# Moving 224 stores of computed results from SyncE's queue to GpSimd's

## The chip, the cores and the metric

The kernel runs on one core of a Trainium2 chip. The metric is the device time of one execution in microseconds; the kernel before takes 2093.06 us, the median of three runs (2092.97 to 2096.44). The engines are TensorE (PE: matmuls; PEld is its weight load, which overlaps), VectorE (DVE), ScalarE (ACT), GpSimd (POOL) and SyncE (SP). DMA transfers are issued from the queue of an engine; this kernel issues from SP and, for some stores, from ACT. SP computes nothing: its queue holds only DMA issues, which it takes in order, each waiting for what it needs.

## The reference

A sequence of 2048 rows of 1024 (plus 16 meta rows in front) goes through one layer of a hybrid decoder in float32:

```python
s = layer_norm(concat(meta, x))                       # 2064 x 1024
u = s @ w_in                                          # conv value, conv gate, q, k, v, r, gate-down
conv_out = silu(layer_norm(causal_conv31(a * sigmoid(gate)) + conv_b))
gla_out  = rms_norm(gla_chunked(q, k, v, log_g)) * silu(r)
s = layer_norm(alpha * s + concat(conv_out, gla_out) @ w_out)
f = square(relu(s @ w_ff1)) @ w_ff2                   # 1024 -> 4096 -> 1024
s = layer_norm(alpha * s + f)                         # output: the 2048 rows after the meta rows
```

## The kernel before, in words

The 2048 rows are four blocks of 512. A float32 product is made of three matmuls: `split` (L189 to L191) copies the high part of an operand on ACT and subtracts it on DVE, which gives a high and a low tile. The kernel is a program of *units* (one product or a few, on PE), each with *loads* (a weight's DMA and its split) that are emitted as many units ahead as there are free slots in a ring of ten weight slots (`wp`), and of *sides* (input normalization, conv, attention, tails), generators that are stepped between units in proportion to the units' costs. A scheduler then gives every engine's instructions their final order and sets the semaphores; each engine works through its own list in order. A tile that is reused waits for the readers and the stores of its last use.

The stages in order of time, from the trace: input normalization, w_in products, gate, conv (on DVE, L723) and attention (0 to 625 us); w_out of blocks 0 and 1 (627 to 705); FF1 of half 0, that is of blocks 0 and 1 (705 to 1035); FF2 of half 0 (1035 to 1345); w_out of blocks 2 and 3 (1376 to 1452); FF1 of half 1 (1452 to 1771); FF2 of half 1 (1771 to 2082), last normalization and the output's stores.

FF1 is done with seven products for eight (a scheme after Strassen). The weight's columns make 16 groups. For groups 0 to 9 two of the seven products are made in advance (the *front*), and their results wait in DRAM (`a1d` and `hor`); in the main part such a group has five products, 6, 5, 7, 3, 4, and `reload` (its DMAs are L1020 and L1022) brings the two results back as `a` and `h`. Groups 10 to 15 have seven products. For each group two pieces of the weight, `w1r` number 0 and 1 (512 KB each, L964), take slots of the ring; DVE combines them in place and splits them (L971, then L191, giving `wop`), and `s`, a third combination, takes a small tile. `wop` of product 4, the last, reads piece 1. After the products DVE (L1034) makes combinations `p`, `u`, `h`, `s` for FF2, and `put` (L1004) stores each into `hor`; FF2 loads them as `lr` (L1125).

What leaves the core's memory in between: `s0d` (normalized input, L304), `hd` (gated conv input, L602, its halo L606, the meta rows L620), `mixd` (attention result `go`, L704, and conv result `cy`, L753), `s1d` (normalized residual, L842, L887) and `hor`. All of these are read back later, by SP loads: `xin` and `wacc` (L833), `hin` (L717), `mraw` (L825), `lr`. Their stores are issued on SP, in the order in which the scheduler puts them; those of `put` that are marked `late` are emitted one unit later than their result by `prog.defer`.

POOL fills constants at the start and makes the power step (x^-0.5, L215 and L243) of every normalization: DVE gives the variance, POOL the power, DVE and ACT apply it, and in the conv normalization PE then transposes (L744) what ACT made (`cn`, L741).

Of the kernel before, what the change touches and what calls it, by code (L numbers as in the profile page):

```python
# [17 lines left out]
P = 128  # L18
# [3 lines left out]
SUB = 512  # L22
# [4 lines left out]
CT = DCONV // P  # L27
# [118 lines left out]
def hymba_kernel(ctx: ExitStack, tc: tile.TileContext, x, meta, ln_in_g, ln_in_b, w_in, small, gate_up,  # L146
# [143 lines left out]
    def prep_tile(s, tt):  # L290
        if s or tt == 0:
            load_x(s, tt)
        t = xin[s, tt]
        if s == 0 and tt == 0:
            nc.sync.dma_start(out=A.g, in_=ln_in_g.partition_broadcast(P))
            nc.sync.dma_start(out=A.b, in_=ln_in_b.partition_broadcast(P))
        yield
        st = stats_bn(t) if s == 0 and tt < NBN else stats_act(t, None, pa, "sg")
        if s == 0 and tt == 0:
            prog.pre(4)  # L300
            load_x(0, 1)
        yield
        yield from ln_apply(t, st, A.g, A.b)
        nc.sync.dma_start(out=s0d[s][tt], in_=t)  # L304
        yield from transpose_split(t, xt[s], tt)
        if s == 0 and tt == 0:
            prog.pre(RING - 4)
            consts()
# [131 lines left out]
    def win_units(s):  # L440
# [157 lines left out]
        def val_evac(i, m, ps):  # L598
            ct = i * 2 + m
            h = pa.tile([P, SUB], F32, tag="h", name="h", bufs=2)  # L600
            nc.vector.tensor_tensor(out=h, in0=ps, in1=sig[ct], op=ALU.mult)
            nc.sync.dma_start(out=hd[s][ct][:, HALO:], in_=h)  # L602
            if s:
                hdone.add((s, ct))
            if s + 1 < NSUB:
                nc.sync.dma_start(out=hd[s + 1][ct][:, :HALO], in_=h[:, SUB - HALO:])  # L606

        sigm = {}

# [5 lines left out]
        def valm_evac(i, m, ps):  # L615
            ct = i * 2 + m
            h = pa.tile([P, HALO], F32, tag="hm", name="hm", bufs=2)
            nc.vector.memset(h[:, :HALO - NMETA], 0.0)
            nc.vector.tensor_tensor(out=h[:, HALO - NMETA:], in0=ps[:, :NMETA], in1=sigm[ct], op=ALU.mult)
            nc.sync.dma_start(out=hd[0][ct][:, :HALO], in_=h)  # L620
            hdone.add((0, ct))

        def gate_val():
# [25 lines left out]
    def gla(s):  # L649
        w = W[s]  # L650
        for c in range(TT):
# [49 lines left out]
                nc.tensor.transpose(tp[:, h * P:(h + 1) * P], og[:, h * P:(h + 1) * P], ident)  # L701
            go = pa.tile([P, 512], F32, tag="go", name="go", bufs=1)
            nc.scalar.activation(go, tp, AF.Identity, scale=sm[:, SM_GG:SM_GG + 1])
            nc.sync.dma_start(out=mixd[s][1][:, :, lo:lo + P], in_=go.rearrange("p (h t) -> p h t", h=NH))  # L704
            yield

    GLA_N = TT * 7
# [3 lines left out]
    def conv(s):  # L711
# [15 lines left out]
        for tt in range(TT):  # L727
            tp = tp_tile()
            for ct in range(CT):
                nc.tensor.transpose(tp[:, ct * P:(ct + 1) * P], accs[ct][:, tt * P:(tt + 1) * P], ident)  # L730
            st = stp.tile([P, 1, 6], F32, tag="cbn", name="cbn")
            nc.vector.bn_stats(st[:, 0], tp)
            mv = stp.tile([P, 2], F32, tag="mv", name="mv")
            nc.vector.bn_aggr(mv, st)
            rs = stp.tile([P, 1], F32, tag="rs", name="rs")
            rstd_of(rs, mv[:, 1:2], 1)
            nm = stp.tile([P, 1], F32, tag="nm", name="nm")
            nc.vector.scalar_tensor_tensor(out=nm, in0=mv[:, 0:1], scalar=-1.0, in1=rs, op0=ALU.mult, op1=ALU.mult)
            yield
            n = cv.tile([P, 512], F32, tag="cn", name="cn", bufs=2)  # L740
            nc.scalar.activation(n, tp, AF.Identity, bias=nm[:, 0:1], scale=rs[:, 0:1])  # L741
            tb = tp_tile()
            for ct in range(CT):
                nc.tensor.transpose(tb[:, ct * P:(ct + 1) * P], n[:, ct * P:(ct + 1) * P], ident)  # L744
            yield
            y = cv.tile([P, 512], F32, tag="cy", name="cy", bufs=1)
            for ct in range(CT):
                nc.scalar.activation(y[:, ct * P:(ct + 1) * P], tb[:, ct * P:(ct + 1) * P], AF.Identity,
                                     bias=sm[:, SM_CLB + ct:SM_CLB + ct + 1], scale=sm[:, SM_CG + ct:SM_CG + ct + 1])
            sg = cv.tile([P, 512], F32, tag="cn", name="csg", bufs=2)  # L750
            nc.scalar.activation(sg, y, AF.Sigmoid)
            nc.vector.tensor_tensor(out=y, in0=y, in1=sg, op=ALU.mult)
            nc.sync.dma_start(out=mixd[s][0][:, :, tt * P:(tt + 1) * P], in_=y.rearrange("p (c t) -> p c t", c=CT))  # L753
            yield

    CONV_N = CT * CW + TT * 3
# [78 lines left out]
    def wout_units(s, late=None):  # L835
        sums = {}

        def post(tt):
            a = wacc[s, tt]
            for _ in ln_apply(a, stats_act(a, sums[tt], rawp, "raw"), B.g1, B.b1):  # L840
                pass
            nc.sync.dma_start(out=s1d[s][tt], in_=a)  # L842
            if tt == 0:
                st1[s] = xt_pair()
            for _ in transpose_split(a, st1[s], tt):
                pass
# [33 lines left out]
    def back_units(half, stats, X):  # L880
# [3 lines left out]
        def norm(tt):  # L884
            t = wacc[b, tt]
            yield from ln_apply(t, stats[tt], B.g1, B.b1)
            nc.sync.dma_start(out=s1d[b][tt], in_=t)  # L887

        def turn(tt):
            t = wacc[b, tt]  # L890
# [51 lines left out]
    def ff1s_units(half, stats, f2):  # L942
# [61 lines left out]
        def put(g, i, t, late=False):  # L1004
            o = hor[half][g // GP][i - 1][:, g % GP, :]
            if late:
                prog.defer(1, lambda: nc.sync.dma_start(out=o, in_=t))
            else:
                nc.scalar.dma_start(out=o, in_=t)

# [361 lines left out]
```

## Time and profile before

| | |
|---|---|
| median of three runs | 2093.06 us |
| the profiled execution | 2097.01 us, span 2095.3 us |
| busy share: PE, PEld, DVE, ACT, POOL | 96%, 79%, 79%, 48%, 4% |
| DMA | 409.39 MB, 195 GB/s over the span |
| weight loads of PE in FF1, half 0 (705 to 1035 us) | 256.74 us of 330 |
| in FF1, half 1 (1452 to 1771 us) | 249.65 us of 319 |
| in FF2, half 0 (1035 to 1345 us) | 251.09 us of 310 |

A busy share is an average over stages with different limits, and PE's matmuls are pipelined, so its 96% still contains short losses; the busy time or the count of its weight loads in a window shows them better. What SP waits for is a wait of a queue: it costs only where something that it issues afterwards comes too late for an engine that then makes PE late. SP, ACT and POOL each take their DMA issues in order.

### The profile page before, as it was taken

To read this page: it belongs to the slowest core of one execution; us is meant where nothing else is said; L and a number is where in the kernel's file an instruction comes from. 1 tells how busy PE (TensorE), PEld (TensorE's weight loads), DVE (VectorE), ACT (ScalarE), POOL (GpSimd) and SP (SyncE) were. 2 spreads that over 40 slices of the span, in tenths; PEclk is the share of its full clock that TensorE was granted. 3 is DMA by queue.
4 is the path that set the end of the run, shared out by engine and by line. 5 is a ranking of instruction groups with operands and counts; after the bars stand their busy time and mean duration, and the time that the engine had idled before them with its cause. 6 is when DMAs were issued, how large, how long until landed. Compare 5 with 4: busy or idle time off the path is not lost. (4 is left out here: it accounts for less than half of the span.)

```text
span 2095.3 us, 26293 instructions
## 1 busy us (share of the span) xinstructions
PE 2021.2 (96%) x9144; PEld 1645.3 (79%) x9144; DVE 1650.6 (79%) x2662; ACT 1002.6 (48%) x1717; POOL 82.1 (4%) x97
## 2 busy tenths in 40 slices
PE   7999999999999999999999999999999999899997
PEld 5878878878777877778788788777777788788886
DVE  6699979989998777776699999579878766544776
ACT  4563474554543554455653434455644554444332
POOL 1000100100000000000000000011000000000001
PEclk9999999999999999999999999999999999999999
DMA  6533534534346656554899877277666548865772
GB/s 204 177 105 93 158 106 122 161 86 134 106 138 209 194 171 217 195 181 161 284 330 389 308 252 269 72 245 251 193 204 204 183 147 283 311 213 188 250 243 79
DMA packets 245285, 409.39 MB, mean 195 GB/s; under 512 B 21424, under 2 KB 115856, under 8 KB 245152
## 3 DMA queue, kind: packets, MB, share of 16 engines
q1 hardware_dynamic: 226144, 368.91, 53.8%
q10 hardware_dynamic: 19008, 38.81, 4.9%
q8 instruction: 72, 1.18, 0.2%
q14 instruction: 61, 0.50, 0.1%
HBM read 297.29 MB, written 110.35 MB: 195 GB/s over the span
## 5 line engine op out<-in xcount | busy, mean ns | idle before, releaser
L723 DVE SCALAR_TENSOR_TENSOR cacc<-hin,sm,cacc 128x512 f32<-128x512 f32 x480 | 344.9, 747 | 2.0
L1211 PE MATMUL mm<-op 128*128 128x512 f32 x544 | 213.6, 393 | 7.5 <-ACT op L190 7.5
L190 ACT CAST wsl<-raw 128x512 fp32r<-128x512 f32 x224 | 136.6, 620 | 164.0 <-PE mm L389 36.5
L1212 PE MATMUL mm<-op 128*128 128x512 f32 x544 | 212.9, 391 | 0.0
L1213 PE MATMUL mm<-op 128*128 128x512 f32 x544 | 211.7, 391 | 0.0
L190 ACT CAST op<-wr 128x1024 fp32r<-128x1024 f32 x92 | 92.4, 1050 | 221.9 <-PE mm L1213 161.4
L191 DVE TENSOR_TENSOR op<-wr,op 128x1024 fp32r<-128x1024 f32 x92 | 109.0, 1221 | 79.4 <-ACT op L190 79.4
L191 DVE TENSOR_TENSOR wsl<-raw,wsl 128x512 fp32r<-128x512 f32 x224 | 150.9, 686 | 21.8 <-ACT wsl L190 21.4
L1000 PE MATMUL gl<-x,wop 128*128 128x512 f32 x384 | 152.2, 398 | 8.0 <-DVE a L1034 2.9
L387 PE MATMUL mm<-xt,wsl 128*128 128x512 f32 x384 | 152.7, 398 | 0.0
L388 PE MATMUL mm<-xt,wsl 128*128 128x512 f32 x384 | 151.3, 394 | 0.0
L389 PE MATMUL mm<-xt,wsl 128*128 128x512 f32 x384 | 151.1, 394 | 0.0
L1001 PE MATMUL gl<-x,wop 128*128 128x512 f32 x384 | 150.6, 392 | 0.0
L1002 PE MATMUL gl<-x,wop 128*128 128x512 f32 x384 | 150.2, 392 | 0.0
L1211 PEld LDWEIGHTS mm<-op 128*128 128x128 f32 x544 | 102.8, 189 | 30.1 <-ACT op L190 8.3
L190 ACT CAST wop<-w1r 128x512 fp32r<-128x512 f32 x152 | 91.1, 616 | 68.5 <-DVE w1r L971 39.8
L1212 PEld LDWEIGHTS mm<-op 128*128 128x128 f32 x544 | 102.8, 189 | 21.3
L1213 PEld LDWEIGHTS mm<-op 128*128 128x128 f32 x544 | 102.4, 188 | 21.7 <-DVE op L191 0.2
L191 DVE TENSOR_TENSOR op<-lr,op 128x1024 fp32r<-128x1024 f32 (+1 forms) x92 | 105.0, 1175 | 16.6 <-ACT op L190 16.5
L191 DVE TENSOR_TENSOR wop<-w1r,wop 128x512 fp32r<-128x512 f32 x152 | 103.8, 687 | 16.3 <-ACT wop L190 15.7
L1000 PE MATMUL mm<-xt,wop 128*128 128x512 f32 x256 | 100.7, 396 | 5.7 <-ACT a L1040 5.7
L1001 PE MATMUL mm<-x,wop 128*128 128x512 f32 x256 | 101.2, 395 | 0.9 <-DVE x L191 0.9
(277 smaller groups left out, 4795.1 us busy)
## 6 DMA issues: line engine op xcount, KB each, us to landing
wr<-in_w_dram SPq DMA_DIRECT2D x120, 512.0 KB, 6.1
lr<-hor SPq DMA_DIRECT2D x108, 512.0 KB, 6.0
raw<-in_w_in_dram SPq DMA_DIRECT2D x160, 256.0 KB, 2.9
w1r<-in_w_dram SPq DMA_DIRECT2D x64, 512.0 KB, 5.2
wr<-td SPq DMA_DIRECT2D x40, 512.0 KB, 5.2
raw<-in_w_out_dram SPq DMA_DIRECT2D x64, 256.0 KB, 3.8
hor<-s SPq DMA_DIRECT2D x64, 256.0 KB, 3.0
raw<-in_w_dram SPq DMA_DIRECT2D x40, 256.0 KB, 3.9
```

Source lines behind the costliest of these rows:

```text
L190: nc.scalar.copy(hi, src)
L191: (eng or nc.vector).tensor_tensor(out=lo, in0=src, in1=hi.bitcast(F32), op=ALU.subtract)
L387: nc.tensor.matmul(ps, wh, mov(k, 0), start=(k == 0), stop=False)
L388: nc.tensor.matmul(ps, wh, mov(k, 1), start=False, stop=False)
L389: nc.tensor.matmul(ps, wl, mov(k, 0), start=False, stop=(k == KD - 1))
L723: nc.vector.scalar_tensor_tensor(out=acc, in0=h[:, j:j + SUB], scalar=wc(j), in1=acc, op0=ALU.mult, op1=ALU.add)
L1000: nc.tensor.matmul(ps, wh, X[i][:, k, 0, :], start=start and k == 0, stop=False, skip_group_check=not start)
L1001: nc.tensor.matmul(ps, wh, X[i][:, k, 1, :], start=False, stop=False, skip_group_check=not start)
L1002: nc.tensor.matmul(ps, wl, X[i][:, k, 0, :], start=False, stop=(k == 3), skip_group_check=not start)
L1211: nc.tensor.matmul(ps, lh, rt[n][:, p, 0, :], start=(q == 0 and p == 0), stop=False)
L1212: nc.tensor.matmul(ps, lh, rt[n][:, p, 1, :], start=False, stop=False)
L1213: nc.tensor.matmul(ps, ll, rt[n][:, p, 0, :], start=False, **ends)
```

## The change

Nine lines that issued a store on SP issue it on POOL: 16 stores `s0d` (512 KB each), 16 `hd` (256 KB), 12 halos, 4 of the meta rows, 16 `go` and 16 `cy` (256 KB), 16 `s1d` (512 KB), and 128 `hor` (256 KB: 64 from `s`, 32 from `u`, 32 from `h`). The last ones are no longer deferred. The stores of the output (L1290, L1292) and the loads stay on SP, and ACT's stores stay on ACT.

```diff
--- before.py
+++ after.py
@@ -301,7 +301,7 @@
             load_x(0, 1)
         yield
         yield from ln_apply(t, st, A.g, A.b)
-        nc.sync.dma_start(out=s0d[s][tt], in_=t)
+        nc.gpsimd.dma_start(out=s0d[s][tt], in_=t)
         yield from transpose_split(t, xt[s], tt)
         if s == 0 and tt == 0:
             prog.pre(RING - 4)
@@ -599,11 +599,11 @@
             ct = i * 2 + m
             h = pa.tile([P, SUB], F32, tag="h", name="h", bufs=2)
             nc.vector.tensor_tensor(out=h, in0=ps, in1=sig[ct], op=ALU.mult)
-            nc.sync.dma_start(out=hd[s][ct][:, HALO:], in_=h)
+            nc.gpsimd.dma_start(out=hd[s][ct][:, HALO:], in_=h)
             if s:
                 hdone.add((s, ct))
             if s + 1 < NSUB:
-                nc.sync.dma_start(out=hd[s + 1][ct][:, :HALO], in_=h[:, SUB - HALO:])
+                nc.gpsimd.dma_start(out=hd[s + 1][ct][:, :HALO], in_=h[:, SUB - HALO:])
 
         sigm = {}
 
@@ -617,7 +617,7 @@
             h = pa.tile([P, HALO], F32, tag="hm", name="hm", bufs=2)
             nc.vector.memset(h[:, :HALO - NMETA], 0.0)
             nc.vector.tensor_tensor(out=h[:, HALO - NMETA:], in0=ps[:, :NMETA], in1=sigm[ct], op=ALU.mult)
-            nc.sync.dma_start(out=hd[0][ct][:, :HALO], in_=h)
+            nc.gpsimd.dma_start(out=hd[0][ct][:, :HALO], in_=h)
             hdone.add((0, ct))
 
         def gate_val():
@@ -701,7 +701,7 @@
                 nc.tensor.transpose(tp[:, h * P:(h + 1) * P], og[:, h * P:(h + 1) * P], ident)
             go = pa.tile([P, 512], F32, tag="go", name="go", bufs=1)
             nc.scalar.activation(go, tp, AF.Identity, scale=sm[:, SM_GG:SM_GG + 1])
-            nc.sync.dma_start(out=mixd[s][1][:, :, lo:lo + P], in_=go.rearrange("p (h t) -> p h t", h=NH))
+            nc.gpsimd.dma_start(out=mixd[s][1][:, :, lo:lo + P], in_=go.rearrange("p (h t) -> p h t", h=NH))
             yield
 
     GLA_N = TT * 7
@@ -750,7 +750,7 @@
             sg = cv.tile([P, 512], F32, tag="cn", name="csg", bufs=2)
             nc.scalar.activation(sg, y, AF.Sigmoid)
             nc.vector.tensor_tensor(out=y, in0=y, in1=sg, op=ALU.mult)
-            nc.sync.dma_start(out=mixd[s][0][:, :, tt * P:(tt + 1) * P], in_=y.rearrange("p (c t) -> p c t", c=CT))
+            nc.gpsimd.dma_start(out=mixd[s][0][:, :, tt * P:(tt + 1) * P], in_=y.rearrange("p (c t) -> p c t", c=CT))
             yield
 
     CONV_N = CT * CW + TT * 3
@@ -839,7 +839,7 @@
             a = wacc[s, tt]
             for _ in ln_apply(a, stats_act(a, sums[tt], rawp, "raw"), B.g1, B.b1):
                 pass
-            nc.sync.dma_start(out=s1d[s][tt], in_=a)
+            nc.gpsimd.dma_start(out=s1d[s][tt], in_=a)
             if tt == 0:
                 st1[s] = xt_pair()
             for _ in transpose_split(a, st1[s], tt):
@@ -884,7 +884,7 @@
         def norm(tt):
             t = wacc[b, tt]
             yield from ln_apply(t, stats[tt], B.g1, B.b1)
-            nc.sync.dma_start(out=s1d[b][tt], in_=t)
+            nc.gpsimd.dma_start(out=s1d[b][tt], in_=t)
 
         def turn(tt):
             t = wacc[b, tt]
@@ -1004,7 +1004,7 @@
         def put(g, i, t, late=False):
             o = hor[half][g // GP][i - 1][:, g % GP, :]
             if late:
-                prog.defer(1, lambda: nc.sync.dma_start(out=o, in_=t))
+                nc.gpsimd.dma_start(out=o, in_=t)
             else:
                 nc.scalar.dma_start(out=o, in_=t)
```

Three places show how the instructions move. First SP's list in the main part of FF1, half 0, in two periods of groups with five products. In the names `hor_0_6_146` is a DRAM tile, `w1r` the weight pieces, `a` and `h` the reloads; in brackets are the semaphores an instruction waits for (DMAHW: an earlier DMA of SP or ACT; DMASW: one of POOL; Activation is ACT). Before:

```order
L1007 DMA hor_0_6_146<-s_7408 128x512 [waits DVE_49]
L1007 DMA hor_0_4_144<-u_7338 128x512 [waits DMAHW7_49,DVE_49]
L964 DMA w1r<-in_w_dram 128x4x256 [waits DMAHW1_49,PE_49]
L1007 DMA hor_0_5_145<-h_7216 128x512 [waits DMAHW2_49,DVE_49]
L1007 DMA hor_0_2_142<-s_7432 128x512 [waits DMAHW3_49,DVE_49]
L964 DMA w1r<-in_w_dram 128x4x256 [waits DMAHW4_49,PE_49,Activation_49]
L1022 DMA h_7576<-hor_1_0_147 128x512 [waits DMAHW5_49,DMAHW2_49]
L1020 DMA a_7814<-a1d_7_219 128x512 [waits DMAHW6_49,DMAHW0_49,Activation_49]
L1007 DMA hor_0_6_146<-s_7528 128x512 [waits DVE_49]
L964 DMA w1r<-in_w_dram 128x4x256 [waits DMAHW1_49,PE_49]
L1007 DMA hor_0_4_144<-u_7458 128x512 [waits DMAHW3_49,DVE_49]
L1007 DMA hor_0_5_145<-h_7336 128x512 [waits DMAHW4_49,DVE_49]
```


After, at the same groups:

```order
L964 DMA w1r<-in_w_dram 128x4x256 [waits DMAHW4_49,PE_49]
L964 DMA w1r<-in_w_dram 128x4x256 [waits DMAHW6_49,DMAHW0_49,DVE_49]
L1020 DMA a_7935<-a1d_8_220 128x512 [waits DMAHW5_49,DVE_49]
L1022 DMA h_7697<-hor_1_0_147 128x512 [waits DMASW6_49]
L964 DMA w1r<-in_w_dram 128x4x256 [waits DMAHW2_49,PE_49]
L964 DMA w1r<-in_w_dram 128x4x256 [waits DMAHW6_49,DMAHW4_49,DVE_49]
L1020 DMA a_8055<-a1d_9_221 128x512 [waits DMAHW3_49,DVE_49]
L1022 DMA h_7817<-hor_1_0_147 128x512 [waits DMASW2_49]
L964 DMA w1r<-in_w_dram 128x4x256 [waits DMAHW0_49,PE_49]
L964 DMA w1r<-in_w_dram 128x4x256 [waits DMAHW4_49,DMAHW2_49,DVE_49]
```


The stores are gone, and of the two `w1r` loads of a group the first waits for PE alone, the second for DVE: for the `wop` of product 4 of the group before, the last reader of the slot that it takes.

Second, DVE's list around the change from one group to the next in the same part. `wop<-w1r,wop` is the low half of a split; the last of them ahead of `s_7746<-w1r` is that of product 4. Before:

```order
L191 TENSOR_TENSOR wop<-s_7626,wop 128x4x128 [waits Activation_49]
L1034 TENSOR_TENSOR h_7456<-u_7578,h_7456 128x512 [waits DMAHW0_49,DVE_49]
L191 TENSOR_TENSOR wop<-w1r,wop 128x4x128 [waits Activation_49]
L1034 TENSOR_TENSOR s_7672<-a_7454,h_7456 128x512 [waits DMAHW3_49,DVE_49,Activation_49]
L1034 TENSOR_TENSOR u_7698<-a_7574,gl 128x512 [waits DMAHW7_49]
L191 TENSOR_TENSOR wop<-w1r,wop 128x4x128
L971 TENSOR_TENSOR s_7746<-w1r 128x512 [waits DMAHW3_49]
L1034 TENSOR_TENSOR p_7719<-p_7719,gl 128x512 [waits DMAHW0_49,PE_49,Activation_49]
L1034 TENSOR_TENSOR p_7719<-p_7719,a_7574 128x512 [waits DVE_49]
L971 TENSOR_TENSOR w1r<-w1r 128x4x128 [waits DMAHW0_49]
```


After:

```order
L1034 TENSOR_TENSOR a_7455<-a_7455,gl 128x512 [waits DVE_49,PE_49]
L1034 TENSOR_TENSOR s_7649<-h_7457,u_7579 128x512 [waits DMASW1_49,Activation_49]
L1034 TENSOR_TENSOR u_7579<-u_7579,p_7599 128x512 [waits DVE_49]
L191 TENSOR_TENSOR wop<-w1r,wop 128x4x128 [waits Activation_49]
L1034 TENSOR_TENSOR h_7457<-u_7579,h_7457 128x512 [waits DMASW6_49,DVE_49]
L191 TENSOR_TENSOR wop<-w1r,wop 128x4x128 [waits Activation_49]
L1034 TENSOR_TENSOR s_7675<-a_7455,h_7457 128x512 [waits DMASW3_49,DVE_49]
L1034 TENSOR_TENSOR u_7699<-a_7575,gl 128x512 [waits DMAHW3_49]
L971 TENSOR_TENSOR s_7746<-w1r 128x512 [waits DMAHW2_49]
L971 TENSOR_TENSOR w1r<-w1r 128x4x128 [waits DMAHW4_49,DVE_49,PE_49]
```


The `wop` of product 4 stood behind the last combination `s` and the next `u`; now it stands ahead of both. The first use of piece 1 (`w1r<-w1r`) stood behind two combinations `p`; now it follows the `s` from `w1r` at once. From one first use of piece 1 to the `wop` of product 4 there are fourteen instructions after the first. Instructions that write a stored tile now wait for a POOL store (DMASW) of an earlier group.

Third, POOL's list in the input stage, at the conv normalization of block 0. Before, power steps alone (`rs` and `rr` are the variances of the normalizations and of the attention):

```order
L215 TENSOR_TENSOR rr<-rr,nhalf 128x4 [waits DVE_49]
L215 TENSOR_TENSOR rs<-rs,nhalf 128x1 [waits DVE_49,Pool_49] x2
L243 TENSOR_TENSOR rs<-rs,nhalf 128x1 [waits DVE_49,Pool_49]
L215 TENSOR_TENSOR rs<-rs,nhalf 128x1 [waits DVE_49,Pool_49]
L215 TENSOR_TENSOR rs<-rs,nhalf 128x1 [waits DVE_49,Activation_49]
L215 TENSOR_TENSOR rr<-rr,nhalf 128x4 [waits DVE_49]
L243 TENSOR_TENSOR rs<-rs,nhalf 128x1 [waits DVE_49]
```


After:

```order
L215 TENSOR_TENSOR rs<-rs,nhalf 128x1 [waits DVE_49,Pool_49]
L753 DMA mixd_0_232<-cy 512x1x128 [waits DMASW2_49,DVE_49]
L215 TENSOR_TENSOR rs<-rs,nhalf 128x1 [waits DVE_49,Pool_49]
L243 TENSOR_TENSOR rs<-rs,nhalf 128x1 [waits DVE_49,Pool_49]
L304 DMA s0d_3_103<-xin 128x1024 [waits DMASW3_49,DVE_49]
L215 TENSOR_TENSOR rs<-rs,nhalf 128x1 [waits DVE_49,Pool_49]
L753 DMA mixd_0_232<-cy 512x1x128 [waits DMASW4_49,DVE_49]
L704 DMA mixd_1_233<-go 512x1x128 [waits DMASW5_49,Activation_49]
L215 TENSOR_TENSOR rs<-rs,nhalf 128x1 [waits DVE_49,Pool_49]
L753 DMA mixd_0_232<-cy 512x1x128 [waits DMASW6_49,DVE_49]
```


The same power steps now stand between stores, each of which waits for the tile that it stores and for the POOL store eight before it.

## Rows read from the trace of the kernel before

**Rows 1.** The page, busy time and share of the span by engine.

```profile
PE 2021.2 (96%) x9144; PEld 1645.3 (79%) x9144; DVE 1650.6 (79%) x2662; ACT 1002.6 (48%) x1717; POOL 82.1 (4%) x97
```

**Rows 2.** Windows: start:end, us; busy time (and count) by engine, clock, DMA share, GB/s.

```profile
850.00:925.00 75.00, 72.53 (x311) 57.72 (x310) 56.57 (x92) 35.91 (x64) 0.00 (x0) 1.00 0.57 193
925.00:1025.00 100.00, 99.93 (x440) 81.13 (x438) 62.13 (x100) 52.62 (x90) 0.55 (x1) 1.00 0.55 186
```

**Rows 3.** Waits of PE: line, releaser: total us, times, longest.

```profile
PE tp L744 <- ACT cn L741: 7.5, 10, 1.4
PE mm L1211 <- ACT op L190: 7.5, 2, 6.1
```

**Rows 4.** Waits of DVE.

```profile
DVE s L971 <- DMA w1r<-in_w_dram: 47.3, 27, 4.1
```

**Rows 5.** Waits of SP's queue.

```profile
SPq L1007 <- DVE s L1034: 188.0, 56, 12.5
...
SPq L964 <- DVE wop L191: 74.1, 11, 10.4
...
SPq L1022 <- DMA hor<-h: 53.3, 17, 4.5
```

**Rows 6.** Timeline of SP in FF1: start, duration, line, operation.

```profile
860.13 0.38 SPq L964 DMA_DIRECT2D w1r<-in_w_dram  x1
...
864.65 0.38 SPq L1007 DMA_DIRECT2D hor<-s  x1
865.13 0.45 SPq L964 DMA_DIRECT2D w1r<-in_w_dram  x1
```

**Rows 7.** Timeline of DVE in the same period; idle time before, with releaser, in brackets.

```profile
866.61 0.69 DVE L971 TENSOR_TENSOR s<-w1r 128x512 f32<-128x512 f32 x1 [2.68 <-DMA w1r<-in_w_dram]
...
870.58 0.69 DVE L971 TENSOR_TENSOR w1r<-w1r 128x512 f32<-128x512 f32 x1 [2.68 <-DMA w1r<-in_w_dram]
...
879.70 0.68 DVE L191 TENSOR_TENSOR wop<-w1r,wop 128x512 fp32r<-128x512 f32 x1
```

**Rows 8.** Timeline of DVE: group 3 and group 10 of half 0.

```profile
792.80 0.69 DVE L971 TENSOR_TENSOR s<-w1r 128x512 f32<-128x512 f32 x1 [2.50 <-DMA w1r<-in_w_dram]
...
895.16 0.69 DVE L971 TENSOR_TENSOR s<-w1r 128x512 f32<-128x512 f32 x1 [0.20 <-DMA w1r<-in_w_dram]
```

**Rows 9.** The line of the `w1r` loads: time from issue to landing.

```profile
DMA to landing us min/median/max: 3.5/5.2/7.4
```

**Rows 10.** Timeline of SP, from FF1 to FF2 in half 1.

```profile
1780.21 0.32 SPq L1007 DMA_DIRECT2D hor<-s  x1
...
1781.11 8.72 SPq L1125 DMA_DIRECT2D lr<-hor  x5
```

**Rows 11.** Timeline of DVE at the same place.

```profile
1785.25 1.23 DVE L1161 TENSOR_TENSOR wr<-wr 128x1024 f32<-128x1024 f32 x1 [5.07 <-DMA wr<-in_w_dram]
```

**Rows 12.** Timeline of ACT, then PE, at w_out of blocks 2 and 3.

```profile
1367.14 2.64 ACT L190 CAST xt<-mraw 128x512 fp32r<-128x512 f32 x4 [8.31 <-DMA mraw<-mixd]
...
1381.38 0.73 PE L860 MATMUL gl<-wsl,xt 128*128 128x512 f32 x2 [1.43 <-ACT wsl L190]
```

**Rows 13.** Timelines of POOL (its longest step), then of one conv normalization.

```profile
186.57 2.05 POOL L215 TENSOR_TENSOR rr<-rr,nhalf 128x4 f32<-128x4 f32 x1 [81.37 <-DVE rr L214]
...
262.18 0.55 POOL L215 TENSOR_TENSOR rs<-rs,nhalf 128x1 f32<-128x1 f32 x1 [9.60 <-DVE rs L214]
...
262.76 0.16 DVE L738 SCALAR_TENSOR_TENSOR nm<-mv,rs 128x1 f32<-128x1 f32 x1 [0.72 <-POOL rs L215]
263.01 0.78 ACT L741 ACTIVATE cn<-tp,nm,rs 128x512 f32<-128x512 f32 x1 [0.78 <-DVE nm L738]
...
263.84 0.33 PE L744 MATMUL tp<-ident,cn 128*128 128x128 f32 x1 [0.75 <-ACT cn L741]
```

**Rows 14.** Timelines of DVE and POOL at the start.

```profile
10.04 1.61 DVE L348 CAST wgd<-qbd 128x96 fp32r<-128x96 f32 x1
...
9.67 0.99 POOL L345 MEMSET at<- 128x512 f32 x2
```


## Prediction

> **What bounds the kernel now.** I read the page first: TensorE (PE) is busy in 96% of the span, so what can be won at most is what PE loses, and a store matters only where its queue makes PE late or stops doing so [rows 1]. A table of windows shows where. In 925 to 1025 us, where every group of FF1 has seven products, PE starts 438 weight loads in 100 us, one per 0.228 us. In 850 to 925 us, mostly groups with five products, it starts 310 in 75 us, one per 0.242 us: 6% is lost there [rows 2]. PE's own waits are short everywhere, 7.5 us in the largest entries [rows 3], but VectorE (DVE) waits 47.3 us for the pieces `w1r` of the FF1 weight, the same stretch seen from the engine that makes PE's operands [rows 4].
>
> Then I read SyncE's queue (SP), which holds all the stores that the change moves. It stood 188.0 us behind stores of `s`, 74.1 us behind the slots of `w1r`, 53.3 us behind stores that had to land before a reload [rows 5]. These are waits of a queue, not of PE, so they are no gain as they stand. One period tells what they do: the load of the first `w1r` (I call it r0) is issued at 860.13 us, right behind a store of `s`, and the second (r1) at 865.13 us, right behind the next store of `s` [rows 6]. DVE uses them at 866.61 and 870.58 us, each after idling 2.68 us for it [rows 7]. So stores do hold loads up, in the groups with five products, and the steady ones start 14.62 us apart ((895.16 − 792.80)/7) [rows 8]. Sixty matmuls at 0.228 us are 13.7 us: 0.92 us per group is the most that PE can get back. There are seven such periods in each half.
>
> **The change, part by part.** 224 stores leave SP for POOL; nothing is added or removed in arithmetic, and the bytes stay.
>
> *FF1, 128 stores.* On SP each group keeps two loads and two reloads. r0 now waits only for PE's product 5 of two groups before, so it is no longer late. r1 is different: the order shows that it waits for the last `wop` of the group before, because it takes the slot of that group's own r1. That is a loop by itself: from DVE's first use of r1 to that `wop` are 14 instructions. DVE issues them 0.608 us apart when it doesn't wait (870.58 to 879.70 us is 15 steps), so 14 steps and one last instruction of 0.68 us are 9.2 us [rows 7]. Then comes the load itself. In the period shown r1 took 865.13 to 870.58, 5.45 us; the view of that line gives 3.5 at least, 5.2 in the median and 7.4 at most [rows 6, 7, 9]. With r0's load gone well ahead, r1 shares the DMA engines with stores and a reload only, so I take 5.05 us, a little under the median. The loop is then 14.25 us. Gain: 14 periods × (14.62 − 14.25) = **−5.2 us**. The bounds are PE's floor, 14 × 0.92 = −12.9 us, and a landing of 6.0 us, a loop of 15.2, +8 us. So the stall moves from r0 to r1, and most of what was lost stays lost.
>
> The first three groups of each half keep the same order on SP, and I cost them at nothing.
>
> *FF1 to FF2.* Ahead of the first loads of FF2, SP issues at 1780.21 us the last store, then a piece `wr`, and from 1781.11 the `lr` loads of `hor`; DVE gets `wr` 5.07 us late [rows 10, 11], and PE pays 6.1 us for it, the longest wait of the entry for line L1211 [rows 3]. The `lr` loads still wait for the last `s` by the reuse of a tile; only the store and `wr` in front go away, 1781.11 − 1780.21 = 0.9 us. Two halves: **−1.8 us** (bounds 0 and −6).
>
> *The last block's `mixd`.* The loads of `mraw` that open w_out of blocks 2 and 3 read what `cy` stored; ACT waits 8.31 us for them at 1367.14, and later PE 1.43 us behind the weights that were queued after them [rows 12]. A store that POOL issues is on a chain to PE here. SP's slot for a store is 0.38 us [rows 6]; POOL's price for issuing one is shown by nothing in this trace. I bound it by 0.38 from below and by the longest small instruction of POOL, 2.05 us, from above [rows 13], and take 1.0, a little under their middle. With a landing later by a few tenths: **+1.3 us** (0 to +3).
>
> *POOL in the input stage, 80 stores, and s1d, 16.* POOL was 4% busy [rows 1] with the small power step of each normalization. Now these steps stand in order behind stores, and a store waits for its tile and occupies POOL. In the conv normalization such a step stands between DVE, ACT and PE: POOL 262.18, DVE 262.76, ACT 263.01, PE 263.84, with PE idle 0.75 us [rows 13]. PE waited 7.5 us in ten of the places like it [rows 3], so there a delay is paid nearly in full. Of the 16 conv chains perhaps a quarter find a store of 1.0 us in the way, half done: 4 × 0.5 = 2.0, and half a microsecond for the other normalizations, which have PE work before them: **+2.5 us** (bounds 0, and 16 × 1.0 = +16 where every chain meets one).
>
> What takes cover: 64 stores per half in FF1 at 1.0 us each are 4 us of POOL per period of 14; nothing else runs on POOL there, and if that cover fails DVE waits for the `s` and `u` tiles that the stores free.
>
> The sum: −5.2 − 1.8 + 1.3 + 2.5 = −3.2 us. The profiled execution took 2097.0 us, 3.9 above the median 2093.06; it becomes 2093.8, and on the scale of the median **2089.9 us**. A difference under 0.2% (4.2 us) can't be told from none, so this lies just inside "no change".
>
> The trace shows two engines holding one another: DVE's small cast, 128×96, took 1.61 us at 10.04 while POOL's fills ran [rows 14], and POOL's power step takes from 0.55 to 2.05 us [rows 13]. The Trainium skill, page "SBUF — State Buffer", section "Who interferes with whom", has a rule that speaks against this change: POOL writes the descriptors of its DMAs, and is locked out while DVE runs an instruction in a two-port mode; it advises SP or ACT as issuer. The rows agree that the two engines meet; no row here shows a store on POOL, so the rule enters as the third rival.
>
> **The rivals.**
>
> *PE becomes the bound in FF1 (faster).* If r1 alone in the queue lands in 4.5 us or less, the loop is at most 13.7 us, PE's floor, and 14 × 0.92 = 12.9 us come back: −12.9 − 1.8 + 1.3 + 2.5 = −10.9, **2082 us**. For it: the shortest landings are 3.5 us [rows 9]. Against: the median is 5.2, and the four stores of a group now start as soon as their results are there, just while r1 is on its way.
>
> *POOL's order holds the normalizations (slower).* One mechanism: a power step stands behind a store whose tile is not ready, or whose issue is long. It decides from the point where the delay exceeds the slack of a chain, 0 for the ten conv places where PE waits already. With all 16 conv chains 0.8 us later (one store in the way) and 1.0 us for each of six others, that is 12.8 + 6 = 18.8 in place of 2.5; −5.2 − 1.8 + 1.3 + 18.8 = +13.1, **2106 us**. For it: POOL's rows after the change alternate steps and stores. Against: the order follows the times at which the work is due, and 80 stores in 600 us are one in 7.5 us.
>
> *Stores on POOL slow DVE or themselves (slower).* If each of the four stores of a group costs DVE what the cast at 10.04 lost, 1.61 − 0.68 (taking DVE's usual instruction, an upper price for so small a cast) = 0.9 us, and half of them fall into r1's loop, it grows by 1.8 us: 14 × 1.8 = +25 on the sum, **2115 us**. For it: rows 14. Against: a step of POOL that ran beside long DVE instructions was itself the one that grew.
>
> *The stores don't matter.* That the change does what it says is shown by the order; but if r1 lands as before in 5.4 us, the loop is 14.6 us and the sum is +2: 2095 us, inside the main case.
>
> **How the numbers follow.** The forecast with its own range 2085 to 2097: 0.48, of it 0.17 below 2088.9. PE the bound: 0.24. POOL's order: 0.20. POOL against DVE: 0.08. Faster by over 0.2%: 0.24 + 0.17 = 0.41; slower: 0.28 less 0.03 for weak forms of it, 0.25; the same 0.34. The range leaves a tenth on each side: from 2079 (PE bound with both changes of stage gaining in full, −1 us each more) to 2107.
>
> **What would show it.** Right: SP's waits behind `s` gone; DVE's wait before `s` from `w1r` near nothing, and its wait before the first `w1r` sum 2 us or more; periods of 14.0 to 14.5 us; the `tp` wait in L744 within 3 us of 7.5. Periods of 13.7 prove the first rival; L744 at 15 us or more, with POOL steps starting late behind stores, the second; DVE instructions longer than 0.69 us beside POOL's stores the third. The forecast is wrong as a whole if r1's load is not what DVE waits for.

## The result, and the profile after

The changed kernel is slower: 2160.28 us, median of four runs (2157.57 to 2164.77), beside 2094.75 us for the kernel before on the same chip; the ratio is 1.0298, with a 95% interval of 1.0279 to 1.0318. The forecast was 2089.9 us, with a range up to 2107.

The page's line of busy times answers to [rows 1]; under it is the queue that the change added:

```profile
PE 2041.2 (95%) x9144; PEld 1656.7 (77%) x9144; DVE 1649.6 (76%) x2662; ACT 1004.6 (47%) x1717; POOL 213.2 (10%) x321
...
q0 software_dynamic: 19200, 63.17, 8.2%
```

PE's busy time rose by 20 us, though its work is the same, and the span by 64.5. Four of the waits of PE follow; two of them answer to [rows 3] (line, releaser: total us, times, longest):

```profile
PE gl L1000 <- DVE p L1034: 38.5, 17, 3.6
PE tp L744 <- ACT cn L741: 12.1, 12, 3.2
...
PE mm L1211 <- ACT op L190: 8.6, 3, 7.7
...
PE gl L860 <- DVE wacc L867: 5.7, 5, 2.5
```

The first is new: 38.5 us in FF1, in line 1000, behind DVE's `p` (0.8 us before). The stages say the same. Each number is the distance between the first or last matmuls of lines 860, 1000 and 1211 in one trace, in us; two stages that no edit reached differ between traces by up to 2.6 us (w_out, 111.6 and 114.2 with the same order), so smaller differences in this table say nothing:

| kernel | input | w_out 0, 1 | FF1 half 0 | FF2 half 0, w_out 2, 3 | FF1 half 1 | rest |
|---|---|---|---|---|---|---|
| before | 593.5 | 111.6 | 328.9 | 412.1 | 324.3 | 324.9 |
| after | 597.3 | 113.7 | 353.3 | 420.1 | 348.3 | 327.1 |

FF1 lost 24.4 and 24.0 us of the 64.5. In its groups with five products the uses of piece 0 now start here (the first and the last of eight, answering to [rows 8]):

```profile
800.65 0.69 DVE L971 TENSOR_TENSOR s<-w1r 128x512 f32<-128x512 f32 x1 [3.51 <-DMA w1r<-in_w_dram]
```

```profile
920.70 0.69 DVE L971 TENSOR_TENSOR s<-w1r 128x512 f32<-128x512 f32 x1 [2.15 <-DMA w1r<-in_w_dram]
```

That is (920.70 − 800.65)/7 = 17.15 us per group, 14.62 before. One period shows how it comes about. SP (start, duration, line, operation; "x2" counts two issues in the stretch, both pieces):

```profile
864.00 1.86 SPq L964 DMA_DIRECT2D w1r<-in_w_dram  x2
...
881.96 1.46 SPq L964 DMA_DIRECT2D w1r<-in_w_dram  x2
```

The second issue of each pair, seen by itself:

```profile
865.48 0.38 SPq L964 DMA_DIRECT2D w1r<-in_w_dram  x1
```

```profile
883.04 0.38 SPq L964 DMA_DIRECT2D w1r<-in_w_dram  x1
```

DVE in the same stretch, answering to [rows 7], to the first use of the next piece 1:

```profile
869.78 0.69 DVE L971 TENSOR_TENSOR s<-w1r 128x512 f32<-128x512 f32 x1 [3.14 <-DMA w1r<-in_w_dram]
872.63 1.42 DVE L971 TENSOR_TENSOR w1r<-w1r 128x512 f32<-128x512 f32 x2 [2.15 <-DMA w1r<-in_w_dram]
873.96 0.68 DVE L1034 TENSOR_TENSOR p<-p,gl 128x512 f32<-128x512 f32 x1
...
879.18 0.69 DVE L1034 TENSOR_TENSOR a<-a,gl 128x512 f32<-128x512 f32 x1 [0.94 <-PE gl L1002]
...
882.32 0.68 DVE L191 TENSOR_TENSOR wop<-w1r,wop 128x512 fp32r<-128x512 f32 x1
...
891.01 1.42 DVE L971 TENSOR_TENSOR w1r<-w1r 128x512 f32<-128x512 f32 x2 [2.08 <-DMA w1r<-in_w_dram]
```

PE in the same stretch, product 4 with its wait and the start of product 5:

```profile
858.16 0.50 PE L1000 MATMUL gl<-x,wop 128*128 128x512 f32 x1 [2.07 <-DVE p L1034]
...
861.02 0.40 PE L1000 MATMUL mm<-x,wop 128*128 128x512 f32 x1
...
874.70 0.80 PE L1000 MATMUL gl<-x,wop 128*128 128x512 f32 x1 [2.39 <-DVE p L1034]
...
878.99 0.39 PE L1000 MATMUL mm<-x,wop 128*128 128x512 f32 x1
```

The reader is to follow one lap. At 864.00 SP issues piece 0, when PE's product 5 has freed its slot, and at 865.48 piece 1, when DVE's `wop` of product 4 of the group before has freed its own. At 869.78 DVE has piece 0, 5.8 us after its issue. Then DVE stands 2.15 us until piece 1 has landed, 7.0 us after its issue, uses it at 872.63, and only then comes to `p`, at 873.96. `p` takes product 7 out of a PSUM bank onto which product 4 is to be added, so PE, whose product 3 has ended, starts product 4 at 874.70 after 2.39 us of waiting. Product 5 follows at 878.99, and frees the slot for the next piece 0 at 881.96. DVE's `a` waits 0.94 us for product 4; the `wop` of product 4 begins at 882.32 and frees the slot for the next piece 1 at 883.04, which DVE first uses at 891.01. Lap: 18.0 us between the loads of piece 0, 18.4 us between the first uses of piece 1. PE wants these pieces only two groups on; what stands behind them in DVE's list is wanted at once.

### The profile page after: what moved, and what is told of

Its sections match the earlier page's. It is cut to its first block, busy times and chain, and to the rows that moved or that the text cites. A ratio compares the mean times of both kernels' runs of the same rounds, so it can differ in the third digit from the quotient of the medians.

```text
span 2159.8 us, 26528 instructions
## 1 busy us (share of the span) xinstructions
PE 2041.2 (95%) x9144; PEld 1656.7 (77%) x9144; DVE 1649.6 (76%) x2662; ACT 1004.6 (47%) x1717; POOL 213.2 (10%) x321
## 5 line engine op out<-in xcount | busy, mean ns | idle before, releaser
L1211 PE MATMUL mm<-op 128*128 128x512 f32 x544 | 214.5, 394 | 9.9 <-ACT op L190 8.6
L1000 PE MATMUL gl<-x,wop 128*128 128x512 f32 x384 | 157.0, 410 | 40.6 <-DVE p L1034 38.5
L1001 PE MATMUL gl<-x,wop 128*128 128x512 f32 x384 | 154.4, 402 | 0.0
L1002 PE MATMUL gl<-x,wop 128*128 128x512 f32 x384 | 154.2, 402 | 0.0
L1211 PEld LDWEIGHTS mm<-op 128*128 128x128 f32 x544 | 103.4, 190 | 33.5 <-ACT op L190 9.8
L1000 PEld LDWEIGHTS gl<-x,wop 128*128 128x128 f32 x384 | 74.3, 194 | 67.6 <-DVE p L1034 46.0
```

The lines of the kernel that those rows point to most:

```text
L1000: nc.tensor.matmul(ps, wh, X[i][:, k, 0, :], start=start and k == 0, stop=False, skip_group_check=not start)
L1001: nc.tensor.matmul(ps, wh, X[i][:, k, 1, :], start=False, stop=False, skip_group_check=not start)
L1002: nc.tensor.matmul(ps, wl, X[i][:, k, 0, :], start=False, stop=(k == 3), skip_group_check=not start)
L1211: nc.tensor.matmul(ps, lh, rt[n][:, p, 0, :], start=(q == 0 and p == 0), stop=False)
```

## The experiments

Every ratio is to the kernel before, run on the same chip in the same hour. Three questions settle the prediction: is it the new order or the stores on POOL as such, what do the stores outside FF1 cost, and was there a gain to be had at all.

**1. FF1's stores alone, and the others alone.** Only line 1007 as in the change, all else as before:

```diff
-                prog.defer(1, lambda: nc.sync.dma_start(out=o, in_=t))
+                nc.gpsimd.dma_start(out=o, in_=t)
```

> Only the 128 stores of FF1 (hor) on POOL, not deferred; the other 96 stores stay on SP. DVE's list in FF1 is that of the changed kernel: the combination p, which frees PE's bank for product 4, stands behind the first use of piece 1. Theory A (the order of DVE: PE waits for p behind the weight loads): FF1's two halves grow by 24 and 23 us as they did with the whole change, so about 2093 + 47 = 2140 us (ratio 1.020 to 1.025). Theory B (POOL's issuing or landing is slow in itself): the cost goes by the number of stores, 128 of 224, 65 x 0.57 = 37 us, 2130 us. Theory C (the conv and attention normalizations held up by stores on POOL make the loss): no more than 2100 us.

Measured: ratio 1.0247 (1.0220 to 1.0274), some 50 us; FF1 took 353.0 and 348.3 us, as with the whole change. Its largest wait of PE is the same line as above:

```profile
PE gl L1000 <- DVE p L1034: 39.7, 17, 3.8
```

Then the eight other lines of the change, with line 1007 as before:

> The 96 other stores (s0d, hd, halo, meta, go, cy, s1d) on POOL; FF1's stores on SP and deferred as before, DVE's list in FF1 as before. Theory A: FF1 as before, periods 14.6 us; what is left is what the input stage, w_out and the block change lost, 4 + 2 + 8 = 14 us: about 2107 us (ratio 1.004 to 1.008). Theory B: 65 x 0.43 = 28 us, 2121 us. Theory C: nearly the whole loss, 2150 us or more.

Measured: ratio 1.0059 (1.0037 to 1.0080), 12 us; FF1 took 333.0 and 322.9 us. The two ratios add up to the whole (1.0247 + 0.0059 = 1.0306, measured 1.0298). Theory B's 28 us for the others, by the number of stores, is too much, and theory C, nearly the whole loss from them, is out.

**2. The deferral alone.** The change to line 1007 does two things. This run does the other:

```diff
-                prog.defer(1, lambda: nc.sync.dma_start(out=o, in_=t))
+                nc.sync.dma_start(out=o, in_=t)
```

> The kernel before with the 128 stores of FF1 still on SP but no longer deferred by a unit: the other half of the change to line 1007. The scheduler gives DVE and SP the same order in FF1 as before. Theory A (what costs is DVE's order after the stores leave SP): no change, 2093 to 2100 us. Theory D (the defer itself did the work: a store issued without it holds SP up): slower by 20 us or more.

Measured: ratio 1.0036 (1.0019 to 1.0053), 7 us, and none of it in FF1 (330.4 and 322.4 us): it is in FF2 of half 0 and w_out of 2 and 3, 419.3 us for 412.1. DVE's list in FF1 was as before. So the deferral is not what FF1 lost; that the order changed at all needs the stores to leave SP's list.

**3. A program one slot shorter.** A first try to get `p` ahead of piece 1 with the stores on POOL, and its control on SP:

```diff
-    prog = Program(RING)
+    prog = Program(RING - 1)
```

> The changed kernel (all 224 stores on POOL) with a program that keeps 9 slots of the ring filled in place of 10, so that each weight is prepared one step later. That puts DVE's p ahead of the first use of piece 1 again, with the stores still on POOL. Theory A: product 4 no longer waits for piece 1, periods in FF1 come down from 16.5 to 18 to about 14.5, the PE wait in line 1000 behind p (38.5 us) goes to under 10; total about 2160 - 40 = 2120 us, or less, apart from what the shorter ring costs, which the same program with the stores on SP shows. Theory B: the periods stay above 16 us and the total above 2150.

> The kernel before (stores on SP) with 9 slots of the ring filled in place of 10: the control for the run with 9 slots and stores on POOL; DVE's list in FF1 is the same in both but for one place. Theory A: with the same order on DVE, stores on POOL are worth no loss in FF1, so the two differ by no more than the 14 us of the other stages. Theory B: this one is faster than the other by 40 us or more. Its own time: weights come one step later, 0 to +20 us on 2093.

Measured: 1.0254 (1.0225 to 1.0283) on POOL and 1.0112 (1.0085 to 1.0140) on SP. Of PE's waits the one behind `p` went from 38.5 us off the list, and `u`, the next combination in DVE's list, took its place with 16.6:

```profile
PE gl L1000 <- DVE u L1034: 16.6, 14, 2.4
```

FF1 fell from 353.3 to 340.1 and from 348.3 to 339.8 us. The shorter ring has a price of its own: on SP FF2 of half 0 with w_out 2, 3 took 432.2 us for 412.1 (on POOL 424.5). The two kernels differ by 0.0142, some 30 us, where theory A allowed 14 and theory B asked for 40 or more; in FF1, with 331.6 and 325.9 us on SP, they differ by 8.5 and 13.9 us, though `p` stands ahead of piece 1 in both. So with this program stores on POOL still cost 22 us in FF1, in a way that was not followed up. The test changed too much at once to decide.

**4. The order on DVE.** Here product 7's unit is emitted ahead of the loads of that step, and the first use of piece 1 is put behind its `p` by an edge of issue order, which makes nothing wait for a result. What is computed, and where the stores are issued, stays; the lists of the other engines shift with it, in FF1 SP's too, and with them the slots that the pieces take:

```diff
-            if i:
+            if i and i not in self.post:
                 self.pre(min(len(self.loads) - self.nxt, self.ring - self.live))
...
             u.fn()
+            if i in self.post:
+                self.pre(min(len(self.loads) - self.nxt, self.ring - self.live))
...
+        def behind():
+            return tc.issue_after(p_ins[0].ins) if p_ins[0] is not None else nullcontext()
+
...
                     if i == 6:
                         tt_(r.s3, r11, r21, ALU.subtract)
-                        tt_(r21, r21, r22, ALU.add)
-                        tt_(r11, r21, r11, ALU.subtract)
+                        with behind():
+                            tt_(r21, r21, r22, ALU.add)
+                            tt_(r11, r21, r11, ALU.subtract)
...
-                tt_(st["p5"], st["p5"], a1[g])
+                p_ins[0] = tt_(st["p5"], st["p5"], a1[g])
...
+                if i == 7 and g < NFR:
+                    prog.post.add(prog.mark())
```

With all 224 stores on POOL:

> The changed kernel (224 stores on POOL), with one edge of issue order: DVE's first use of weight piece 1 stands behind the p of the product 7 before it, as in the kernel before; the s from piece 0 still stands ahead of p. Nothing is computed otherwise. Theory A: PE's wait behind p (38.5 us) falls to under 15, the periods of FF1 to about 14.6, and the time to that of the other 96 stores alone plus little: 2108 to 2118 us. Theory B (stores on POOL slow in themselves): 2145 us or more.

Measured: ratio 1.0096 (1.0069 to 1.0124) in place of 1.0298: this edit gives back two thirds of the loss, and FF1 takes 335.4 and 323.9 us. No wait of PE behind `p` is left on its list. With FF1's stores alone on POOL:

> Only FF1's 128 stores on POOL, the other 96 on SP, and DVE's first use of piece 1 held behind p. If the whole loss of the FF1 stores (50 us) came from DVE's order, 2095 to 2100 us, and with steady periods at 14.0 us, as the run with all stores on POOL and the same edge showed in half 1, 2088 to 2098. If a store on POOL has a price of its own in FF1, 2105 us or more.

Measured: ratio 1.0025 (1.0011 to 1.0040), where the same stores without the edge gave 1.0247. So nine tenths of what FF1's stores cost, 45 of 50 us, goes with the order, and POOL as issuer is left with 5. The edit moved two things, though: `p` ahead of piece 1, and the slot that piece 1 takes. What SP waits for before its load shows the second, in the changed kernel (794 to 918 us; eight loads of each piece), then with the edge (1535 to 1641 us):

```profile
SPq L964 <- PE mm L1002: 82.1, 8, 12.1
...
SPq L964 <- DVE wop L191: 7.3, 8, 1.8
```

```profile
SPq L970 <- PE gl L1009: 26.2, 8, 4.0
```

There piece 1 waited for DVE's `wop` of product 4; here it waits for a product of PE, and comes to be issued 3.2 to 4.5 us behind piece 0, in place of 1.0 to 2.2. It landed in 4.8 to 6.3 us, in place of 6.7 to 8.2. No run moves one of the two without the other.

FF1 of half 1 took 320.1 us. Its steady groups, the first and the last of seven (one of those between waited 0.29 us for a piece, the others for none):

```profile
1555.51 0.68 DVE L977 TENSOR_TENSOR s<-w1r 128x512 f32<-128x512 f32 x1
```

```profile
1639.92 0.68 DVE L977 TENSOR_TENSOR s<-w1r 128x512 f32<-128x512 f32 x1
```

(1639.92 − 1555.51)/6 = 14.07 us per group, and 14.64 before ((1639.01 − 1536.54)/7). Half 0 of the same run had no such gain: 14.74 us per group ((896.90 − 793.73)/7) for 14.62, and 332.1 us for 328.9. Windows of the same length say what PE does in them (start:end; busy time and count by engine; clock, DMA share, GB/s). The kernel before, in half 1:

```profile
1530.00:1700.00 170.00, 166.92 (x717) 133.44 (x716) 129.50 (x207) 83.06 (x148) 0.00 (x0) 1.00 0.60 198
```

The changed kernel:

```profile
1530.00:1700.00 170.00, 151.07 (x629) 118.23 (x627) 117.26 (x187) 73.12 (x131) 17.31 (x32) 0.97 0.55 180
```

FF1's stores on POOL, with the edge:

```profile
1530.00:1700.00 170.00, 169.06 (x731) 136.80 (x731) 134.21 (x215) 87.17 (x152) 25.40 (x47) 1.00 0.59 197
```

PE started 716, 627 and 731 weight loads in the 170 us (the times are the same, not the groups: FF1 of half 1 began 38 us later in the changed kernel, so its stretch holds more groups with five products). The last is the gain that the prediction looked for, 2% of that stretch; the middle is what came.

The same with all three uses of the pieces, the `s` too, behind `p`, for all stores on POOL, for FF1's alone, and for the kernel before:

> The same with all three uses of the pieces, the s too, behind p. Product 4 then waits for no weight load. Theory A: periods at or below 14.6 us, down to PE's 13.7, since the loads are needed a whole group later than p: 2098 to 2112 us. If DVE's next result for PE (u of product 3), which now stands behind piece 1, takes p's place as the wait, the periods stay near 15 and the time near 2120.

> The same with all three uses of the weight pieces behind p. If order alone made the loss: 2088 to 2100 us, perhaps below the kernel before. If a store on POOL has a price of its own: 2105 us or more.

> The kernel before (stores on SP, deferred) with the same three uses behind p. Theory A: the wait of product 4 for the s, and through it for piece 0, goes; SP's stores still hold the loads, so the gain is a part of the 0.9 us per group that PE loses there: 2085 to 2093 us. If p was not what PE waited for in the kernel before: 2093 to 2100.

Measured: 1.0102 (1.0077 to 1.0127), 1.0037 (1.0022 to 1.0052) and 0.9992 (0.9976 to 1.0009). The `s` in front of `p` costs nothing that can be seen: of the two pieces, piece 1 is the one that matters here. Order without POOL gains nothing measurable in all either; but in that last kernel, with every store on SP, FF1 took 328.1 and 320.7 us, and PE started 727 weight loads from 1530 to 1700 us. So the shorter FF1 of half 1 comes with the order and needs no store on POOL.

**5. The other stores.** The attention's and the conv's (`go`, `cy`: lines 704 and 753 of the change), then the input's (`s0d`, `hd`, halo, meta: lines 304, 602, 606, 620), each with all else as before:

> Only go and cy (32 stores, the ones that stand between the power steps of the conv normalization and of the attention) on POOL, all else as before. If these are what costs in the other 96 stores (11 us): 2104 to 2110 us, most of it in the input stage and in w_out of blocks 2 and 3. If not: 2094 to 2100.

> Only s0d, hd, its halo and the meta rows (48 stores) on POOL, all else as before. If what costs is POOL's occupation by stores as such: about half of the 11 us, 2099 to 2105. If it is cy and go alone: 2094 to 2098.

Measured: 1.0030 (1.0016 to 1.0043) and 1.0003 (0.9989 to 1.0017). So the 32 stores among the power steps cost about 6 us, and the 48 others nothing. Some 6 of the 12 us of experiment 1 are left, and `s1d` was not tried by itself. Where the 6 us fall is not settled: input and w_out are 3.6 us longer each in that trace, little over what equal stages differ by (w_out was 3.5 us longer too with FF1's stores alone on POOL, which are issued after it); of PE's waits the one for `wacc` in w_out rose, from 2.5 to 7.0 us:

```profile
PE gl L860 <- DVE wacc L867: 7.0, 3, 3.0
```

**6. Half 1 alone.** If the shorter FF1 of half 1 is real, it should show with everything before it left in place. Both kernels have the edge of experiment 4 in half 1 as well; the second has, besides, all three uses behind `p` in half 0, which cost nothing on SP:

```diff
-                prog.defer(1, lambda: nc.sync.dma_start(out=o, in_=t))
+                if half:
+                    nc.gpsimd.dma_start(out=o, in_=t)
+                else:
+                    prog.defer(1, lambda: nc.sync.dma_start(out=o, in_=t))
...
```

> Up to FF1 of half 1 the kernel before, word for word in its order. In half 1 alone FF1's 64 stores go to POOL, with DVE's first use of piece 1 held behind p. If the gain is real: FF1 of half 1 takes 320 us in place of 324, all earlier stages as before, in all 2089 us on the scale of 2093 (ratio 0.997 to 0.9985). If the shorter stage in the earlier run was luck of its order: no change (0.9990 to 1.0015).

> The same in half 1, and in half 0 the stores on SP with all three uses of the weight pieces behind p, which took 328.1 for 328.9 us. If both are real: 2088 us on the scale of 2093 (ratio 0.9965 to 0.998). If not: no change.

Measured: 0.9995 (0.9982 to 1.0007) and 0.9991 (0.9979 to 1.0004). FF1 of half 1 took 322.7 and 321.2 us for 324.3. The steady groups of half 1 do run at 14.1 us, so the gain per group is there, but it is 2 to 3 us in all, and neither kernel beats the one before by more than can be measured.

## Why the prediction was wrong

**The step that failed** is the first term, FF1's 128 stores at −5.2 us; it came out at +48 in the changed kernel (24.4 and 24.0) and +50 by itself. The loop that the prediction drew, from DVE's first use of r1 (piece 1) to the last `wop` and back through r1's load, did close: in the eight steady groups of half 0 each load of r1 waited for that `wop` (the eight waits in experiment 4). Wrong were the load in it, taken at 5.05 us and 6.0 at most, and that nothing was put in for PE behind `p`.

First, r0 (piece 0) was to be "no longer late" and "gone well ahead". But r0 waits for PE's product 5 "of two groups before", and DVE works two groups ahead of PE: SP stood before these eight loads for 82.1 us, until that product ended. Taking the stores away could not bring r0 forward. It was so before the change, too: in the period of [rows 6] SP's last wait before r0's load, at 859.5 us, was for PE and not for the store:

```profile
SPq L964 <- PE mm L1002: 0.6, 1, 0.6
```

Second, r0 and r1 so travelled together. In the lap followed above the DMA engines were busy to 0.97 and 0.99 from r0's issue until r1 had landed:

```profile
864.40:869.70 5.30, 5.30 (x25) 4.22 (x24) 2.25 (x4) 0.72 (x2) 1.28 (x3) 1.00 0.97 323
869.70:872.50 2.80, 2.61 (x12) 1.79 (x10) 0.69 (x1) 0.00 (x0) 0.00 (x0) 1.00 0.99 352
```

r1 took 7.0 us there, and 6.7 to 8.2 in the eight groups; the prediction had r1 "with stores and a reload only". From its first use to the next issue DVE's 14 instructions took 9.4 to 10.5 us for the 9.2 forecast, the longer ones with a wait for product 4. The loop had 17.56 us on average ((925.72 − 802.81)/7) in place of 14.25.

Third, the rows of the order showed what else had moved: the two `p` stood ahead of the first use of piece 1, and now stood behind it. The prediction's front part says so, and its sum doesn't ask who waits for `p`. PE does, for the bank of product 4, 38.5 us in all. That ties PE to DVE's loop at once, and makes the loop longer where DVE then waits for a late product 4 (0.94 us at 879.18).

The seven steady laps of each half, 17.15 and 17.28 us ((1696.88 − 1575.89)/7) for 14.62 and 14.64, make 36 of the 48 us; the others fall before and behind them and were not traced further. How much of it is the longer landing, and how much PE's waiting for `p`, stays open: the edge took both away.

What the prediction gave as the sign of being wrong as a whole, that piece 1 is not what DVE waits for, didn't occur: DVE did wait for it, 41.9 us. The loop was the right one; the sign could not tell that a term in it was too small, nor who stood behind DVE.

**A lower clock made it worse.** After the wait of 2.39 us the granted clock fell; windows of that place in the changed kernel, and one from the next lap:

```profile
858.00:860.00 2.00, 1.84 (x8) 1.54 (x9) 2.00 (x5) 1.88 (x4) 0.00 (x0) 1.00 0.00 0
872.00:874.60 2.60, 0.31 (x2) 0.00 (x0) 1.94 (x4) 0.48 (x1) 0.00 (x0) 0.96 0.36 126
874.60:876.00 1.40, 1.30 (x3) 1.11 (x4) 1.40 (x4) 1.30 (x4) 0.00 (x0) 0.50 0.00 0
876.00:878.00 2.00, 2.00 (x6) 1.54 (x6) 2.00 (x4) 1.94 (x4) 0.00 (x0) 0.55 0.00 0
878.00:880.00 2.00, 2.00 (x10) 1.61 (x10) 1.06 (x3) 0.46 (x2) 0.00 (x0) 1.00 0.35 131
...
893.00:896.00 3.00, 2.92 (x13) 2.42 (x14) 3.00 (x7) 2.88 (x6) 0.00 (x0) 1.00 0.00 0
```

PE in the next lap:

```profile
893.09 0.50 PE L1000 MATMUL gl<-x,wop 128*128 128x512 f32 x1 [2.83 <-DVE p L1034]
...
895.94 0.40 PE L1000 MATMUL mm<-x,wop 128*128 128x512 f32 x1
```

In the two windows up to 878 us it stood at 0.50 to 0.55, PE's lower level of 1.2 GHz, and product 4 took 878.99 − 874.70 = 4.3 us; after the wait of 2.07 us at 858.16 it stayed at 1.00 and product 4 took 861.02 − 858.16 = 2.9. So the fall cost that lap 1.4 us on top of the wait. The length of the wait did not decide it: after 2.83 us, at 893.09, the clock stayed at 1.00 and product 4 took 895.94 − 893.09 = 2.9 us. Of the eleven waits behind `p` of over 2 us in both halves, six came with a fall; by an estimate from these six products 4 against 2.85 us each, the clock makes some 10 of the 48 us. In the windows of half 1 in experiment 4 it was 0.97, where it was 1.00 before.

**The other terms.** The store's price on POOL, bounded by 0.38 and 2.05 us and taken at 1.0, was 0.54 in FF1 and 0.73 for `cy` in the median; POOL in the period shown, and at a conv normalization:

```profile
863.32 0.54 POOL L1007 DMA_DIRECT2D hor<-s  x1 [12.96 <-DVE s L1034]
864.05 0.54 POOL L1007 DMA_DIRECT2D hor<-u  x1 [0.19 <-issue]
865.25 0.54 POOL L1007 DMA_DIRECT2D hor<-h  x1 [0.67 <-DVE h L1034]
866.46 0.55 POOL L1007 DMA_DIRECT2D hor<-s  x1 [0.67 <-DVE s L1034]
```

```profile
269.68 0.75 POOL L753 DMA_DIRECT2D mixd<-cy  x1 [6.30 <-DVE rs L214]
270.42 0.58 POOL L215 TENSOR_TENSOR rs<-rs,nhalf 128x1 f32<-128x1 f32 x1
```

The power step at 270.42 starts as the store ends, so the second rival's mechanism can occur. Its price was not paid there in sum: DVE's waits for the power step in the conv normalization came to 10.3 us for 10.1 before. L744's wait rose from 7.5 to 12.1 us, +4.6 for the +2.5 of the sum, in the changed kernel; with `go` and `cy` alone it was 8.2, so the rise is not shown to be theirs. The block change (+1.3) and these steps together stand against the 12 us of the 96 stores: mis-sized by a factor of three. The −1.8 us from FF1 to FF2 did not come: the longest wait in L1211 went from 6.1 to 7.7.

**The rivals.** The third (POOL's stores slow DVE) is out: beside POOL's stores DVE's instructions kept their 0.68 to 0.69 us (below, one that ran during the store at 865.25), and the Trainium skill's lock ("SBUF — State Buffer", "Who interferes with whom") is not seen here. FF1's list has no copies or casts on DVE, only instructions of two tensors, so this says nothing of the modes that the rule names.

```profile
865.37 0.68 DVE L1034 TENSOR_TENSOR s<-a,h 128x512 f32<-128x512 f32 x1
```

Landing is another matter: the stores of line 1007 took 3.5 us in the median on SP and 4.6 on POOL, the loads of `w1r` 5.2 and 5.8; line 1007 and line 964 of the changed kernel:

```profile
DMA to landing us min/median/max: 2.3/4.6/7.6
```

```profile
DMA to landing us min/median/max: 3.5/5.8/8.8
```

What POOL as issuer adds to a landing was not isolated; with the edge in place it is within the 5 us that remain. The first rival (PE the bound in FF1) did not come with the change. With the edge half 1 came near it, 14.07 us per group for its 13.7, half 0 did not.

**What stays open.** Why the scheduler chose the new order was not measured. With ten slots and no edge it gave the same one whenever FF1's stores left SP, and the old one whenever they stayed, with and without the deferral; the likely reason is that it judges the pieces to land earlier once no store is listed ahead of them. The stage between FF1 of half 0 and of half 1 was 3.4 to 9.5 us longer in nearly every kernel in which stores of half 0 left SP or lost their deferral (419.3 us even without POOL), with FF1's order changed or not; its cause was not looked for.

## What to carry to other kernels

Taking work off a queue also changes what the scheduler believes to be ready first, and so the order of engines that the edit doesn't name. Before a wait is counted as a gain, go through each instruction that has changed places with it on an in-order engine, and ask who waits for that one: here two additions, 0.68 us each, carried a bank of PE. And before a load is given the landing time that it had, ask what is issued beside it now: here two loads that had been 2.3 to 5.0 us apart in half 0 left within 2.2 us of each other. If an order matters, state it as an edge of issue order, rather than leave it to the times at which data happen to come.

## What was not expected of the hardware

PE's clock fell to its lower level at a single wait of 2.39 us in a stretch that was otherwise busy, and the 1.4 us that this cost are more than half of the wait itself; at a wait of 2.83 us in the next lap it did not fall. And a store costs no more on POOL to issue (0.54 us for 256 KB in rows of 2 KB) than the shortest power step that POOL makes besides (0.55 to 2.05 us, [rows 13]).
